# Convolution taps shared between VectorE and TensorE, norms applied two chunks at a time, and weight splits taken off GpSimd, in a six-layer transformer kernel

## The chip, the cores and the metric

The kernel runs on one core of a Trainium2 chip. The metric is device time in microseconds of one launch. Before the change three runs gave 2338.33, 2335.90 and 2334.93 us, a median of 2335.9 us. One more execution was taken with the hardware profiler; all durations below come from it.

## What is computed

256 tokens of 1024 channels pass through two blocks. The first has four layers of attention (differential, latent, dilated, differential) with a SwiGLU network each; nothing of it changes here. The second has two layers, and these are the subject. A layer, cut to what matters:

```
def token_mix(h, positions, w_in, ...):
    z = h @ w_in + b_in
    u_pool, u_conv, q, k, v, qi, ki, wi, gates = split_cols(z, IN_SIZES)
    ...
    y_pool = pool_mixer(u_pool, pool_w, pool_scale) @ w_pool_out
    y_conv = conformer_conv(u_conv, conv_dw_w, conv_dw_b, conv_ln_g, conv_ln_b, w_conv_out)
    y_attn = dsa_attention(q, k, v, qi, ki, wi) @ w_attn_out
    g = jax.nn.sigmoid(gates).reshape(B, L, 3, D_MODEL)
    merged = g[:, :, 0] * y_pool + g[:, :, 1] * y_conv + g[:, :, 2] * y_attn
    return merged @ w_o

def conformer_conv(u, dw_w, dw_b, ln_g, ln_b, w_pw):
    a, gate = jnp.split(u, 2, axis=-1)
    h = causal_dwconv(a * jax.nn.sigmoid(gate), dw_w, dw_b)   # 31 taps, 256 channels
    return jax.nn.silu(layer_norm(h, ln_g, ln_b)) @ w_pw

def conv_ffn(h, w_up, ffn_dw_w, ffn_dw_b, w_down):
    u = causal_dwconv(h @ w_up, ffn_dw_w, ffn_dw_b)           # 3 taps, 5632 channels
    gate, val = jnp.split(u, 2, axis=-1)
    return (jax.nn.silu(gate) * val) @ w_down

h = layer_norm(ALPHA * h + token_mix(h, ...), ln1_g, ln1_b)
h = layer_norm(ALPHA * h + conv_ffn(h, ...), ln2_g, ln2_b)
```

In the attention each query keeps its 64 highest-scored keys (score from 8 index heads).

## The kernel before, in words

**Layout and products.** Activations are held transposed: eight chunks of 128 channels on the partitions, 256 tokens along the free axis. Every product is made of three matmuls (`mm3`): each fp32 operand is split into a high part (rounded to the matmul's input type) and a low part (the rest), and high x high, high x low and low x high are added in PSUM. Weights come in pieces. For each piece SP's queue starts a DMA into one of 5 `raw` buffers, ScalarE copies it to `whi` (L243, the recording helper), VectorE subtracts to get `wlo` (L315); there are 6 buffers of each part. Some pieces are split by GpSimd, by an argument of `weights`.

**Order.** A scheduler gives each engine its instructions in an order fixed at build time. In the token mixer TensorE runs the main pieces in the order of the program; side steps (index scores, top-k, softmaxes, the convolution's norm) are put in a list with `later(delay)`, and are emitted when a virtual clock, which every main step advances with `tick`, has passed their due time. So the delays decide where side steps stand among the gate pieces, on all engines.

**Entry.** `normed` starts the layer: the statistics of the layer norm are ready late, so the first two weight pieces are multiplied with the un-normed input (z), and afterwards mended with the norm's scale and shift (`early`, L1247 and L1248). Meanwhile `ln_apply` (L1103) norms the eight chunks: per chunk two VectorE operations, a ScalarE copy to the high part, one VectorE operation for the low part. The bias of the norm is added to the kept x later, in the token mixer by eight ScalarE operations (at j == 2), in the FFN by eight GpSimd ones (L1149).

**Token mixer** (`token_mix`, L1304). After the entry: queries of the index (`zqi`), a packed piece with keys, values and index weights (`zb`), queries (`zq`); a bias row `bz` is fetched by ScalarE's queue for each (L1318) and added when the result leaves PSUM (L1333, L1358). Then two pieces for the pool branch, four for the convolution's input and its gate, then 20 gate pieces (j = 2 to 11, two each). Transposes of keys (`zkd`), 8 index products, 8 rounds of top-k on VectorE (L1409, L1410) and 8 softmax steps (`attend`) are side steps. The 31 taps of the convolution run on TensorE between the gate pieces j = 3 to 6: the input, padded in front (`cvp`), is shuffled so that even and odd tokens share the partitions, and each of four packed pieces of tap weights (times two halves) has 16 calls of `mm3` with 128 columns, 64 calls a layer.

**FFN** (`conv_ffn`, L1609). 22 pairs of pieces j, 48 matmuls of 256 columns for each j. The result is copied from PSUM (`upr`, ScalarE, 128x512), one ScalarE and two VectorE operations per half make the three taps (`gut`), and a product with a SiLU gives `guh`. The pieces j = 2 to 6 have one of their two splits on GpSimd.

Of the kernel before, what the change touches and what calls it, by code (L numbers as in the profile page):

```python
# [25 lines left out]
CW = 31  # L26
# [4 lines left out]
NPOOL, NH = 7, 18  # L31
# [70 lines left out]
def prepare(i):  # L102
# [39 lines left out]

    dw = f(i["conv_dw_w_2"]).reshape(2, CW, 2, 2, 64)
    tp = np.zeros((2, 2, 64, 16, 2, 2, 2, 64), np.float32)
    for e in range(2):
        for sh in range(2):
            for d in range(16):
                for o in range(2):
                    j = 2 * d + sh - o
                    if 0 <= j < CW:  # L150
                        for c in range(64):
                            tp[:, sh ^ e, c, d, :, e, o, c] = dw[:, j, :, e, c]
    a["w_tap"] = tp.reshape(2, 128, 4, 2048).transpose(0, 2, 1, 3)
# [17 lines left out]
    for l in range(2):  # L171
# [3 lines left out]
        p.add(f"psc{l}", cols(f(i["pool_scale_2"])[l]))  # L175
        p.add(f"cb{l}", cols(f(i["conv_dw_b_2"])[l]))
# [42 lines left out]
class Program:  # L219
# [153 lines left out]
    def setup(self):  # L373
# [6 lines left out]
        for h, eng in ((0, nc.sync), (1, nc.scalar)):  # L380
            x = c.tile([128, 4, 256], F32, name=f"x{h}")
            eng.dma_start(x, xv[:, 4 * h:4 * h + 4, :])
            self.x += [x[:, k, :] for k in range(4)]
        self.ident = self.col("ident", 0, 128)
# [692 lines left out]
    def spread(self, mean, sq, eps, extra=None):  # L1077
# [20 lines left out]
        ra, bb = self.t1("lna"), self.t1("lnb2")  # L1098
        self.act(ra, self.bcast(r))
        nc.vector.tensor_copy(bb, self.bcast(b))  # L1100
        return ra, bb

    def ln_apply(self, x, ra, bb, g, b):  # L1103


        xs = self.splits()
        for k in range(8):
            gk, bk = self.col(g, k), self.col(b, k)
            self.stt(x[k], x[k], gk, ra, OP.mult, OP.mult)
            self.stt(x[k], bb, gk, x[k], OP.mult, OP.add)  # L1110
            self.act(xs[k][0], x[k], AF.Identity, bias=bk)
            self.stt(xs[k][1], x[k], bk, xs[k][0].bitcast(F32), OP.add, OP.subtract)
        return xs
# [31 lines left out]

    def bias(self, b):

        for k in range(8):
            self.nc.gpsimd.tensor_scalar(self.x[k], self.x[k], self.col(b, k), None, op0=OP.add)  # L1149
# [78 lines left out]
    def normed(self, st, aps, take):  # L1228


        ra, bb = self.stats(st)
# [6 lines left out]
        xs = self.ln_apply(self.x, ra, bb, st["g"], st["b"])  # L1238
# [14 lines left out]
    def angles(self):  # L1253
# [40 lines left out]
        self.cvp = c.tile([128, 2, 287], F32, name="cvp")  # L1294
# [9 lines left out]
    def token_mix(self, l, st):  # L1304
# [111 lines left out]
        self.later(3.0, lambda: keys(0, kiT))  # L1416
        for hh in range(8):
            self.later(5.5 + 1.5 * hh, lambda hh=hh: index(hh))
        self.later(18.0, attended)
# [52 lines left out]
        wide_ = lambda: self.rslot().rearrange("p a b -> p (a b)")[:, :574].rearrange("p (f n) -> p f n", f=2)  # L1472
        nh, nl = wide_(), wide_()
        self.split(nh, nl, cvp, 1.0)
        taps = []
        for n in (nh, nl):
            o = self.rslot().rearrange("p a b -> p (a b)")[:, :572].rearrange("p (f e n) -> p f e n", f=2, e=2)
            for e in range(2):
                own, other = slice(64 * e, 64 * e + 64), slice(64 - 64 * e, 128 - 64 * e)
                self.act(o[own, :, e, :], n[own, :, 0:286:2].bitcast(F32))  # L1480
                self.act(o[other, :, e, :], n[own, :, 1:287:2].bitcast(F32))
            taps.append(o)
# [54 lines left out]
        for c in range(4):  # L1537
            es = {}
            for e in range(2):
                self.later(8.0 + 6.0 * (2 * c + e), lambda c=c, e=e, es=es: attend(c, e, es))  # L1540
# [3 lines left out]
        cv = []  # L1544
        for j in range(2, 12):
# [4 lines left out]
            if 3 <= j < 7:  # L1550
                b = j - 3
# [125 lines left out]
```

## Time and profile before

| | us |
|---|---|
| median of three runs | 2335.9 |
| the profiled execution | 2332.99 |
| its span in the profile | 2330.9 |
| TensorE busy | 2246.2 |
| VectorE busy | 1638.5 |
| ScalarE busy | 1358.0 |
| GpSimd busy | 271.8 |
| second block, first layer: z ends | at 1473.7 |
| its gates end | at 1632.2 |
| its FFN: z ends | at 1705.1 |

The clock granted to TensorE over the whole span was 0.986 of full speed. In the rows, PE is TensorE, DVE VectorE, ACT ScalarE, POOL GpSimd and SP SyncE; L12 is line 12 of the kernel. A matmul's own duration overlaps the next, so the pace is read from a chain of them (us and count). "idle before <-releaser" is the time in which the engine did nothing ahead of an instruction, and what ended it.

### The profile page before, as it was taken

To read this page: it belongs to the slowest core of one execution; us is meant where nothing else is said; L and a number is where in the kernel's file an instruction comes from. 1 tells how busy PE (TensorE), PEld (TensorE's weight loads), DVE (VectorE), ACT (ScalarE), POOL (GpSimd) and SP (SyncE) were. 2 spreads that over 40 slices of the span, in tenths; PEclk is the share of its full clock that TensorE was granted. 3 is DMA by queue.
4 is the path that set the end of the run, shared out by engine and by line. 5 is a ranking of instruction groups with operands and counts; after the bars stand their busy time and mean duration, and the time that the engine had idled before them with its cause. 6 is when DMAs were issued, how large, how long until landed. Compare 5 with 4: busy or idle time off the path is not lost.

```text
span 2330.9 us, 43099 instructions
## 1 busy us (share of the span) xinstructions
PE 2246.2 (96%) x16822; PEld 2111.3 (91%) x16822; DVE 1638.5 (70%) x2914; ACT 1358.0 (58%) x2470; POOL 271.8 (12%) x257
## 2 busy tenths in 40 slices
PE   8999998999999999999999999899999998998998
PEld 6899997899977778999978999789999997998998
DVE  6776666776556656766677767785888788578875
ACT  7764456544556656644577545565558565555763
POOL 1010012300010000100002002010152001005311
PEclk9999999999999999999999999999999999998999
DMA  6345553355554343455633656444445554443543
GB/s 231 131 156 187 157 174 112 114 191 159 185 189 137 115 140 126 151 184 159 203 128 121 203 164 195 156 145 139 161 144 197 159 190 145 154 166 123 199 157 106
DMA packets 113723, 370.12 MB, mean 159 GB/s; under 512 B 12656, under 2 KB 15856, under 8 KB 113520
## 3 DMA queue, kind: packets, MB, share of 16 engines
q1 hardware_dynamic: 111120, 363.84, 47.5%
q10 hardware_dynamic: 2256, 3.28, 0.5%
q8 instruction: 132, 2.16, 0.4%
q14 instruction: 71, 0.58, 0.1%
q0 software_dynamic: 144, 0.26, 0.1%
HBM read 366.54 MB, written 1.05 MB: 158 GB/s over the span
## 4 chain that ended last, share of the span: by engine, by line
PE 60%; DVE 7%; ACT 2%; issue 1%; DMA 1%; POOL 0%; ACTq 0%; DVEq 0%; SPq 0%; POOLq 0%
PE mm L272 51%; PE sc L272 6%; PE tp L326 2%; DVE xl L246 1%; DVE wlo L315 1%; DVE x L246 1%; ACT whi L243 1%; ACT s L243 1%; PE tp L272 1%; DMA raw<-w_zq 0%; DVE early L1248 0%; DVE score L1410 0%; PE tp L1061 0%; DMA bz<-b_z 0%; PE tp L714 0%
## 5 line engine op out<-in xcount | busy, mean ns | idle before, releaser
L315 DVE TENSOR_TENSOR wlo<-raw,whi 128x1024 fp32r<-128x1024 f32 (+3 forms) x742 | 842.4, 1139 | 374.5 <-ACT whi L243 373.2
L243 ACT ACTIVATE whi<-raw 128x1024 fp32r<-128x1024 f32 (+2 forms) x760 | 739.1, 978 | 540.2 <-PE mm L272 354.0
L272 PE MATMUL mm<-xh,whi 128*128 128x256 f32 x2496 | 710.1, 285 | 5.6 <-DVE early L1247 5.6
L272 PE MATMUL mm<-xh,wlo 128*128 128x256 f32 x2496 | 704.8, 283 | 3.9 <-DVE wlo L315 3.9
L272 PE MATMUL mm<-xl,whi 128*128 128x256 f32 x2496 | 705.0, 282 | 3.0 <-DVE xl L246 2.9
L272 PE MATMUL mm<-s,whi 128*128 128x256 f32 x2976 | 544.7, 284 | 0.0
L272 PEld LDWEIGHTS mm<-xh,whi 128*128 128x128 f32 x2496 | 474.1, 190 | 8.2 <-DVE early L1247 6.0
L272 PEld LDWEIGHTS mm<-xl,whi 128*128 128x128 f32 x2496 | 474.0, 190 | 4.6 <-DVE xl L246 4.0
L272 PEld LDWEIGHTS mm<-xh,wlo 128*128 128x128 f32 x2496 | 472.9, 190 | 5.3 <-DVE wlo L315 5.3
L272 PEld LDWEIGHTS mm<-s,whi 128*128 128x128 f32 x2976 | 465.4, 192 | 5.0 <-issue 3.8
L272 PE MATMUL mm<-s,wlo 128*128 128x256 f32 x1488 | 421.2, 284 | 0.0
L272 PEld LDWEIGHTS mm<-s,wlo 128*128 128x128 f32 x1488 | 285.3, 192 | 0.1
L272 PE MATMUL mm<-whi,xh 128*128 128x512 f32 (+3 forms) x608 | 246.1, 406 | 13.6 <-ACT whi L243 8.9
L272 PE MATMUL mm<-wlo,xh 128*128 128x512 f32 (+3 forms) x608 | 239.7, 394 | 0.2
L272 PE MATMUL mm<-whi,xl 128*128 128x512 f32 (+3 forms) x608 | 237.7, 391 | 0.0
L272 PEld LDWEIGHTS mm<-whi,xh 128*128 128x128 f32 x608 | 116.4, 192 | 36.1 <-ACT whi L243 8.9
L272 PEld LDWEIGHTS mm<-whi,xl 128*128 128x128 f32 x608 | 115.9, 191 | 22.4
L272 PEld LDWEIGHTS mm<-wlo,xh 128*128 128x128 f32 x608 | 116.1, 191 | 20.4 <-DVE wlo L315 1.8
L486 POOL TENSOR_TENSOR sqacc<-sqacc,sq 128x256 f32<-128x256 f32 x56 | 58.0, 1036 | 585.3 <-ACT sq L243 582.6
L243 ACT ACTIVATE s<-guh 128x256 fp32r<-128x256 f32 x132 | 54.8, 415 | 116.9 <-DVE guh L538 94.2
L534 DVE TENSOR_TENSOR gut<-mm,rbc 128x512 f32<-128x512 f32 x88 | 60.5, 691 | 40.1 <-PE mm L272 40.1
L246 DVE SCALAR_TENSOR_TENSOR gut<-upr,pk,gut 128x255 f32<-128x255 f32 (+1 forms) x160 | 78.4, 518 | 12.1 <-ACT gut L243 10.1
(314 smaller groups left out, 2651.5 us busy)
## 6 DMA issues: line engine op xcount, KB each, us to landing
raw<-w_gu SPq DMA_DIRECT2D x176, 512.0 KB, 4.7
raw<-w_up SPq DMA_DIRECT2D x88, 512.0 KB, 4.2
raw<-w_zs SPq DMA_DIRECT2D x60, 512.0 KB, 3.8
raw<-w_out SPq DMA_DIRECT2D x64, 384.0 KB, 3.2
raw<-w_cqk SPq DMA_DIRECT2D x48, 512.0 KB, 4.4
raw<-w_out SPq DMA_DIRECT2D x64, 320.0 KB, 2.8
raw<-w_aqk SPq DMA_DIRECT2D x32, 512.0 KB, 4.5
raw<-w_cv SPq DMA_DIRECT2D x24, 512.0 KB, 3.7
```

The lines of the kernel that those rows point to most:

```text
L243: return self.nc.scalar.activation(out, in_, func, bias=bias, scale=scale, **kw)
L246: return self.nc.vector.scalar_tensor_tensor(out, a, s, b, op0=op0, op1=op1)
L272: i = self.nc.tensor.matmul(*a, **kw)
L315: e.tensor_sub(lo, raw, hi.bitcast(F32))
L326: i = self.nc.tensor.transpose(out, in_, self.ident if ident is None else ident)
L486: self.nc.gpsimd.tensor_add(acc, acc, sq)
L534: nc.vector.tensor_mul(t, ps, rb[:, None, :].to_broadcast([128, 2, 256]))
```

## The change

Four parts.

1. **Taps.** Of the convolution's two chunks of 128 channels the first goes to VectorE: one ScalarE operation and 30 multiply-adds of 128x256 a layer, queued in threes with `later(6 + 4n)`. The second stays on TensorE, as 31 products with diagonal matrices (`w_tap`, now 4 pieces a layer for 8), 256 columns each, at j = 3 and j = 5. The shuffles to even and odd, and the eight copies that undid them, go.
2. **Norms.** `ln_apply` takes two chunks at a time: VectorE multiplies and adds 128x512, reading scale and shift from PSUM, where they had been copied out; ScalarE applies gain and bias (twice: to the high part and to x); VectorE subtracts once for both low parts. The separate bias additions (ScalarE's and GpSimd's) go.
3. **FFN.** The copy `upr` goes, the taps read PSUM; no split is done on GpSimd.
4. **Delays.** Keys at 9.0 (3.0), index head n at 11.2 + 1.3n (5.5 + 1.5n), top-k's end at 24 (18), softmax steps from 11 (8), the convolution's norm from 16 after j = 5 (3.5 after j = 6).

```diff
-        ra, bb = self.t1("lna"), self.t1("lnb2")
-        self.act(ra, self.bcast(r))
-        nc.vector.tensor_copy(bb, self.bcast(b))
-        return ra, bb
+        return self.bcast(r, b)
...
-        for k in range(8):
-            gk, bk = self.col(g, k), self.col(b, k)
-            self.stt(x[k], x[k], gk, ra, OP.mult, OP.mult)
-            self.stt(x[k], bb, gk, x[k], OP.mult, OP.add)
-            self.act(xs[k][0], x[k], AF.Identity, bias=bk)
-            self.stt(xs[k][1], x[k], bk, xs[k][0].bitcast(F32), OP.add, OP.subtract)
+        rb, bb = (ps[:, None, n:n + 256].to_broadcast([128, 2, 256]) for n in (0, 256))
+        for m, x2 in enumerate(self.x2):
+            self.nc.vector.tensor_mul(x2, x2, rb)
+            self.nc.vector.tensor_add(x2, x2, bb)
+            for to in (lambda k: xs[k][0], lambda k: self.x[k]):
+                for k in (2 * m, 2 * m + 1):
+                    self.act(to(k), self.x[k], AF.Identity, scale=self.col(g, k), bias=self.col(b, k))
+            two = slice(2 * m, 2 * m + 2)
+            self.nc.vector.tensor_sub(self.xl[:, two, :256], x2, self.xh[:, two, :256].bitcast(F32))
...
-        xs = self.ln_apply(self.x, ra, bb, st["g"], st["b"])
+        xs = self.ln_apply(rb, st["g"], st["b"])
+        rs = self.t2("lnrb")
+        self.act(rs, rb)
+        ra, bb = rs[:, :256], rs[:, 256:]
...
-        self.later(3.0, lambda: keys(0, kiT))
+        self.later(9.0, lambda: keys(0, kiT))
         for hh in range(8):
-            self.later(5.5 + 1.5 * hh, lambda hh=hh: index(hh))
-        self.later(18.0, attended)
+            self.later(11.2 + 1.3 * hh, lambda hh=hh: index(hh))
+        self.later(24.0, attended)
...
+        cv = [self.t1("cv") for _ in range(2)]
+        taps = self.rslot().rearrange("p a b -> p (a b)")[:, :572].rearrange("p (s n) -> p s n", s=2)
+        self.split(taps[:, 0, :], taps[:, 1, :], cvp[:, 1, :], 1.0)
+        wcol = lambda t: self.col(f"cw{l}", t)
+        self.act(cv[0], cvp[:, 0, 0:256], AF.Identity, scale=wcol(0), bias=self.col(f"cb{l}", 0))
+
+        def tapped(t0):
+            for t in range(t0, t0 + 3):
+                self.stt(cv[0], cvp[:, 0, t:t + 256], wcol(t), cv[0], OP.mult, OP.add)
+
+        for n in range(10):
+            self.later(6.0 + 4.0 * n, lambda n=n: tapped(1 + 3 * n))
...
-            if 3 <= j < 7:
-                b = j - 3
+            if j in (3, 5):
+                b = (j - 3) // 2
...
-                for k in range(16):
-                    d, n = 4 * b + k // 4, k % 4
-                    at = slice(d, d + 128)
-                    self.mm3(tap[:, n // 2, n % 2, :], w(k, 0), [x[:, n // 2, n % 2, at] for x in taps],
-                             d == 0 and n == 0, d == 15 and n == 3, skip_group_check=True)
-                    self.tick(0.19)
+                for k in range(16 - b):
+                    d = 16 * b + k
+                    self.mm3(tap, w(k, 0), [taps[:, n, d:d + 256] for n in range(2)], d == 0, d == CW - 1)
+                    self.tick(3 * US[256])
...
-                w = self.weights(up[l, j], 256, (nc.vector, nc.gpsimd) if j < NPOOL else None)
-                ps = self.smode2(w, xs)
-                t = self.t2("upr", (2, 256))
-                self.act(t, ps)
-                p = [t[:, f, :] for f in range(2)]
+                ps = self.smode2(self.weights(up[l, j], 256), xs)
+                p = [ps[:, f, :] for f in range(2)]
```

What the scheduler makes of it stands at three places of the second block's first layer. The first is ScalarE's queue at the entry of the token mixer, where `bz` is the bias row. Before, its DMA was issued inside the FFN of the first block:

```order
L243 ACTIVATE whi<-raw 128x640
L243 ACTIVATE gus<-gut 128x256
L243 ACTIVATE s_14432<-guh 128x256
L243 ACTIVATE whi<-raw 128x768
L243 ACTIVATE whi<-raw 128x640
L1318 DMA bz<-b_z 128x512
L243 ACTIVATE gus<-gut 128x256
```

And now, where x_74 are the last four chunks, `lnrb` scale and shift of the norm, `gb` and `shift` what mends the early pieces, and s_16819 the first gates:

```order
L236 ACTIVATE xh<-x_74,pk_122 128x256 x2
L236 ACTIVATE x_74<-x_74,pk_122 128x256 x2
L236 ACTIVATE lnrb<-tp 128x512
L236 ACTIVATE gb<-sc 128x2 x2
L236 ACTIVATE shift<-lnrb,gb 128x256 x3
L236 ACTIVATE s_16819<-early,hb 128x256 x2
L236 ACTIVATE gb<-mm 128x2
L1309 DMA bz<-b_z 128x512
```

The issue of `bz` has moved behind the norm's sixteen operations, the shifts and two of the gates.

The second place is VectorE at the end of top-k, where `mx` are the maxima of a round, `wlo` the low half of a weight piece, `cvp` the convolution's input. Before, the tail of top-k:

```order
L1410 MATCH_REPLACE score<-mx_17595,score 128x128
L1409 MAX mx_17598<-score 128x8
L315 TENSOR_TENSOR wlo<-raw,whi 128x1024
L1410 MATCH_REPLACE score<-mx_17598,score 128x256
L1469 TENSOR_SCALAR glu<-glu 128x256
L246 SCALAR_TENSOR_TENSOR score<-score,causal 128x384
L246 SCALAR_TENSOR_TENSOR cvp<-mm,pk_122,glu 128x256
L1414 TENSOR_SCALAR selb<-score 128x384
L435 TENSOR_TENSOR ropet<-qtok,rt 128x8x32
L436 TENSOR_TENSOR ropet<-qtok,rt 128x8x32
L315 TENSOR_TENSOR wlo<-raw,whi 128x1024
```

And now:

```order
L1401 MATCH_REPLACE score<-mx_17649,score 128x256
L429 TENSOR_TENSOR ropet<-qtok,rt 128x8x32
L239 SCALAR_TENSOR_TENSOR score<-score,causal 128x384
L430 TENSOR_TENSOR ropet<-qtok,rt 128x8x32
L1405 TENSOR_SCALAR selb<-score 128x384
L431 TENSOR_TENSOR qtok<-qtok,rt 128x512
L1460 TENSOR_SCALAR glu<-glu 128x256
L432 TENSOR_TENSOR qtok<-qtok,ropet 128x512
L239 SCALAR_TENSOR_TENSOR cvp<-mm,pk_122,glu 128x256
L308 TENSOR_TENSOR wlo<-raw,whi 128x1024
L447 TENSOR_TENSOR s_17695<-cvp,s_17695 128x286
```

The split of the third gate piece (j = 2), which is the `wlo` of this excerpt, now comes behind the whole of top-k, both ropes of the queries and both gated products; the split ahead of it stands 71 instructions earlier, among the index scores, so there is none inside top-k.

The third place is VectorE at the first softmax step, where `aexp` are the masked scores and `arec` the reciprocal of their sum. Before:

```order
L315 TENSOR_TENSOR wlo<-raw,whi 128x1024 x2
L446 ISA aexp,amax<-sc,selb 128x128
L446 ISA amax 128x1
L446 ISA aexp,amax<-sc,selb 128x256
L446 ISA amax 128x1
L315 TENSOR_TENSOR wlo<-raw,whi 128x1024 x2
L1511 RECIPROCAL arec<-asum 128x2
```

And now:

```order
L239 SCALAR_TENSOR_TENSOR cv<-cvp,pk_122,cv 128x256 x2
L440 ISA aexp,amax<-sc,selb 128x128
L440 ISA amax 128x1
L440 ISA aexp,amax<-sc,selb 128x256
L440 ISA amax 128x1
L239 SCALAR_TENSOR_TENSOR cv<-cvp,pk_122,cv 128x256 x5
L1503 RECIPROCAL arec<-asum 128x2
L239 SCALAR_TENSOR_TENSOR cv<-cvp,pk_122,cv 128x256
L1505 TENSOR_SCALAR aexp<-aexp,arec 128x128
```

Between mask and reciprocal, two weight splits stood at this step and five of the convolution's multiply-adds (`cv`) stand now, with a sixth ahead of the normalising.

## Rows read from the trace of the kernel before

**Rows 1.** The page, busy time, share of span, instructions.
```profile
PE 2246.2 (96%) x16822; PEld 2111.3 (91%) x16822; DVE 1638.5 (70%) x2914; ACT 1358.0 (58%) x2470; POOL 271.8 (12%) x257
```
**Rows 2.** Windows: length, busy time (count) by engine, clock, DMA share, GB/s.
```profile
1473.70:1537.60 63.90, 56.62 (x336) 49.65 (x334) 54.07 (x151) 32.23 (x56) 8.17 (x16) 0.95 0.41 136
1537.60:1632.20 94.60, 90.64 (x734) 86.05 (x735) 55.70 (x108) 60.56 (x117) 1.64 (x5) 0.98 0.49 166
1705.10:1722.50 17.40, 13.81 (x98) 12.99 (x96) 17.40 (x25) 10.33 (x22) 14.93 (x9) 0.90 0.29 99
1903.00:1964.40 61.40, 55.82 (x336) 49.68 (x334) 52.41 (x146) 31.28 (x54) 8.17 (x16) 0.97 0.43 142
1964.40:2057.90 93.50, 89.08 (x734) 85.19 (x735) 55.70 (x108) 60.68 (x117) 0.71 (x1) 1.00 0.48 167
2131.30:2149.10 17.80, 12.07 (x99) 11.46 (x97) 17.80 (x24) 9.79 (x19) 16.73 (x11) 0.97 0.29 98
1499.40:1506.20 6.80, 3.51 (x9) 2.67 (x10) 3.85 (x14) 0.76 (x2) 0.00 (x0) 0.50 0.85 264
```
**Rows 3.** Timeline of TensorE, token mixer's entry: start, us, what, idle before.
```profile
1499.53 0.45 PE L326 MATMUL tp<-pk,zkd 128*128 128x128 f32 x1 [2.28 <-DVE zkd L1361]
1503.14 0.47 PE L326 MATMUL tp<-pk,zkd 128*128 128x128 f32 x1 [3.16 <-DVE zkd L1361]
...
1537.62 0.39 PE L272 MATMUL mm<-xh,wlo 128*128 128x256 f32 x1 [0.42 <-DVE wlo L315]
```
**Rows 4.** The chain of waits in the gates: start, us, engine and line, count.
```profile
1553.31 1.29 PE sc L272 x12
...
1554.95 4.63 PE sc L272 x40
...
1623.02 9.04 PE mm L272 x76
```
**Rows 5.** Groups by form, VectorE from 1723 to 2000; last two, whole span.
```profile
L315 DVE TENSOR_TENSOR wlo<-raw,whi 128x1024 fp32r<-128x1024 f32 x65 | 81.2, 1253 | 18.7 <-ACT whi L243 18.7
L246 DVE SCALAR_TENSOR_TENSOR gut<-upr,pk,gut 128x255 f32<-128x255 f32 x40 | 20.6, 523 | 5.5 <-ACT gut L243 5.5
...
L246 DVE SCALAR_TENSOR_TENSOR x<-x,pk,lna 128x256 f32<-128x256 f32 x8 | 3.6, 474 | 0.0
...
L437 DVE TENSOR_TENSOR qtok<-qtok,rt 128x512 f32<-128x512 f32 x4 | 2.7, 681 | 0.0
L1333 DVE TENSOR_TENSOR qtok<-mm,bz 128x512 f32<-128x512 f32 x4 | 2.6, 682 | 0.0
...
L246 DVE SCALAR_TENSOR_TENSOR s<-s,mm x48: 411/414/422, 1640.5 to 2087.2; 128x256 f32<-128x256 f32 x48
...
L534 DVE TENSOR_TENSOR gut<-mm,rbc 128x512 f32<-128x512 f32 x88 | 60.5, 691 | 40.1 <-PE mm L272 40.1
```
**Rows 6.** DMA issues of the bias row: count, KB each, median us to landing.
```profile
bz<-b_z ACTq DMA_DIRECT2D x4, 256.0 KB, 5.5
```
**Rows 7.** Timeline of VectorE, top-k of the first layer.
```profile
1521.83 0.61 DVE L1409 MAX8 mx<-score 128x8 f32<-128x128 f32 x2
...
1532.83 1.20 DVE L315 TENSOR_TENSOR wlo<-raw,whi 128x1024 fp32r<-128x1024 f32 x1
...
1534.03 0.40 DVE L1410 MATCH_REPLACE8 score<-mx,score 128x256 f32<-128x256 f32 x1
```
**Rows 8.** Timeline of TensorE, third pair of pieces (j = 4), both FFNs.
```profile
1722.51 0.39 PE L272 MATMUL mm<-xh,whi 128*128 128x256 f32 x1 [0.95 <-DVE early L1247]
...
2149.09 0.58 PE L272 MATMUL mm<-xh,whi 128*128 128x256 f32 x1 [4.62 <-DVE early L1247]
```
**Rows 9.** Timelines of VectorE and GpSimd, early pieces of the first FFN.
```profile
1716.65 2.54 DVE L246 SCALAR_TENSOR_TENSOR gut<-early,pk,gut 128x254 f32<-128x254 f32 x1
1719.11 2.62 DVE L1248 TENSOR_TENSOR early<-early,shift 128x256 f32<-128x256 f32 x1
...
1716.54 4.91 POOL L315 TENSOR_TENSOR wlo<-raw,whi 128x1024 fp32r<-128x1024 f32 x2
```

## What the change does to the time, predicted

> **What bounds the kernel now.** I read the page first: TensorE is busy for 96% of the span [rows 1], so a gain has to take work or idle time from it, and the other engines count only where it waits for them. The change leaves the first four layers alone, so the table by stretches comes next, with one row for each stretch of the second block that the change touches [rows 2]. In each row the reader is to take the length and TensorE's busy time. Entry of the token mixer: 63.90 us with 56.62 busy in its first layer, 61.40 with 55.82 in its second. Gates: 94.60 with 90.64, and 93.50 with 89.08. The two early pieces of the FFN: 17.40 with 13.81, and 17.80 with 12.07. So gates are bound by TensorE's work, and entries by what it waits for. [...] When the third gate piece starts, at 1537.62, it waits only 0.42 us for its low half: top-k has just let VectorE go.
>
> **The taps.** Before, a layer has 64 calls of three matmuls of 128 columns, 192. In the chain of waits 12 take 1.29 us and 36 of them with 4 score products 4.63 us [rows 4]: 107 and 116 ns each; at 113 ns, 21.7 us a layer. After, the second chunk has 31 calls, 93 matmuls of 256 columns. 76 of that width take 9.04 us [rows 4], 119 ns each, so 93 take 11.1 us. The first chunk costs TensorE nothing. **Gain 10.6 us a layer**, all on the path, since TensorE bounds the gates; bounds 192 x 0.107 - 93 x 0.121 = 9.3 and 192 x 0.116 - 11.1 = 11.2. So half the columns cost nine tenths of the time, and the change halves the number of matmuls. [...]
>
> VectorE pays for the first chunk with 30 operations of 128x256 a layer. They read SBUF, as the FFN's tap operations do (523 ns [rows 5]) and the norm's (474 ns [rows 5]): 30 x 0.42 to 0.5, 12.6 to 15 us. The gates have VectorE busy for 55.70 of 94.60 us [rows 2]; four tap pieces fewer take 4 x 1.25 off [rows 5], so it comes to 63 to 66 of some 84 us. That fits, if nothing urgent stands behind the new ones. Something does: in the changed order five and then one of them stand between a softmax's mask and its normalising. About 2.4 us come into a chain that needs some 1.4 us without them; TensorE has 42 matmuls, 5 us, before it asks for the result. Cost taken: nothing; the cover lasts until the return is over 1.3 us later still.
>
> **The entry of the token mixer.** TensorE's own work is the busy time less what half clock adds: 56.62 - 1.8 (3.51 busy us at 0.50, [rows 2]) = 54.9 us, and about as much in the second layer. What it lost was 9.0 us and 6.5 us. These waits go: the keys, due at 9 for 3, are transposed after 39 of the 48 matmuls that stand there, so the 2.28 and 3.16 us have cover.
>
> Three waits come. (a) ScalarE issues the DMA of the bias row behind sixteen norm operations, where it had been issued in the FFN before. From issue to landing is 5.5 us [rows 6]. [...] (b) Behind the two additions (682 ns each [rows 5]) VectorE does seven rope operations before it splits the next weights: 3.1 us. (c) **Top-k.** From its first maximum (1521.83) to its last replacement (1534.43) VectorE takes 12.6 us, with one weight split of 1.20 us inside [rows 7]. In the changed order no split stands there: eight rounds with the small ropes (12.6 - 1.2 = 11.4), both halves' query ropes (each two operations of 681 ns [rows 5] and two of half that size, 4.0), then the split (1.2); the two gated products, masks and last scores I put at 3 (some nine operations of 0.25 to 0.5, the norm's 474 ns being the nearest row [rows 5]): 19 to 20 us after the last index product. TensorE has 105 matmuls and six transposes until it wants that split, 13.3 us. Wait 6.4 us; from 3, if the scores come early, to 8. Behind each of the two longer waits I put a half-clock stretch as the row shows it, 1.8 us lost.
>
> So the entry takes 54.9 + 2.6 + 3.1 + 6.4 + 3.6 = 70.6 us, against 63.9 and 61.4: **a loss of 6.7 and 9.2 us**. Bounds for a layer: 60 (waits 3 in all) and 76.
>
> **The norms.** For two chunks VectorE had six operations of 474 ns [rows 5], of which 0.08 overlaps the next, and now has three of 128x512; the nearest row with a PSUM operand is 691 ns [rows 5]. Eight chunks: 12 x 0.65 = 7.8 for 24 x 0.4 = 9.6 us. ScalarE gets eight more, about 0.4 us each, beside them. In the token mixer this lies in the entry above. In the FFN the third piece pair (j = 4) starts 17.4 and 17.8 us after the end of z [rows 2], having waited 0.95 and 4.62 us [rows 8], for 96 matmuls that need 11.5. Two VectorE operations there take 2.54 and 2.62 us while GpSimd splits weights for 4.91 us [rows 9], where such operations take 474 to 523 ns [rows 5]; that goes with the split on GpSimd, some 4.2 us. Put back on VectorE, each split costs 1.25 us [rows 5], and the one for j = 4 stands in the changed order behind twelve tap operations. Norm to 1708.6, early pieces and taps 9 us, split: ready at 1718.9, for 1722.51. **Gain 3.2 us an FFN**, after 0.4 for a longer half clock; bounds nothing and 5.9.
>
> **The FFN's other pieces.** The copy of 128x512 out of PSUM goes from ScalarE, and four tap operations read PSUM themselves. An operation with a PSUM operand of that size (`s<-s,mm`) takes 414 ns [rows 5], less than the 523 ns from SBUF, so no price. Per piece VectorE has two splits, four taps and a product, some 5 us at most, under TensorE's 48 x 0.12 = 5.8. Taken: nothing; it lasts until VectorE needs 0.8 us more a piece. [...]
>
> **Sum.** Taps 2 x 10.6 = 21.2, entries -15.9, FFNs +6.4: 11.7 us. The half-clock stretches were added to the waits as if they never fell on idle time; I give 1.8 us of the 7.2 back, which makes 13.5. The profiled execution takes 2333.0 us, so 2319.5; the median of the three runs is 2.9 us above it, 2335.9, and the forecast for the median is **2322 us**.
>
> **Rivals.**
> *Waits smaller.* The 105 matmuls under top-k hold transposes of late keys and queries; if TensorE's work there covers VectorE after all, (c) and its half clock fall away in both layers: 2 x 8.2 = 16 us more, 2306; with (a) gone too, 2300. For it: 0.42 us of wait before. Against it: there the scores came 6 us earlier, and one split stood inside.
> *Gain given back.* The order is moved but TensorE's starts are bound as before: the taps' 21 us are eaten by entries at their upper bound (76 us: 12 and 15 us lost). 21.2 + 6.4 - 27 = 0.6: 2335. That includes the case that the change does nothing.
> *VectorE bounds the gates: slower.* Place: the tap operations between mask and normalising. Price: above 1.3 us of delay every microsecond is TensorE's in each of the 16 softmax chains, eight a layer. If six more operations of 0.5 us, with one split of 1.25, stand before the result, it is 4.2 - 1.3 = 2.9 us a chain, 46 us in all; with half of the chains hit, 23: 2336 + 23 - 13.5 = 2345. It takes over from 0.85 us a chain on. For it: VectorE goes from 59% to 77% of the stretch. Against it: 5 us of cover and 18 us of idle.
>
> **Chances.** No change I call within 0.2% (4.7 us), about what a measurement can tell. The forecast has 0.50 (2312 to 2331), smaller waits 0.26 (2296 to 2312), gain given back 0.15 (2331 to 2341), VectorE the bound 0.09 (above 2341). Faster 0.76, same 0.15, slower 0.09. The range leaves out the better half of a case on top and the slower one: 2302 to 2336.
>
> **What would show it.** The tap groups: 186 matmuls of 256 columns at 119 ns. Entry rows: transposes of the keys with no wait, a wait for the bias row's addition, and one of 5 to 7 us for the low half at the third gate piece. Gates: 82 to 86 us. FFN pieces: j = 4 starts 14 us after z. The prediction is wrong in its largest term if the entry is shorter than 64 us, and in kind if TensorE waits in the gates for softmax results.

## The result, and the profile after

The changed kernel takes **2312.26 us** (median of 4 runs, 2311.30 to 2312.77), against 2335.99 (4 runs): a ratio of 0.9897, 95% interval 0.9879 to 0.9914, so 1.0% faster, 23.7 us. The forecast was 2322 with a range of 2302 to 2336: the sign and the range held, and the gain was under-estimated, 13.9 us forecast. The median lies at the better edge of the forecast's own band (2312 to 2331), 10 us from its middle. The profiled execution of the changed kernel took 2312.77 us with a span of 2310.9, 20.0 under the span before. The two executions do not start the second block together: the first block, which is the same in both, ended 0.6 us later after the change. So the stages are compared one by one.

Busy time, from the page of the changed kernel:

```profile
PE 2225.8 (96%) x16624; PEld 2094.2 (91%) x16624; DVE 1629.7 (71%) x2924; ACT 1325.3 (57%) x2410; POOL 225.5 (10%) x231
```

TensorE's busy time fell by 20.4 us, which is all of the span's gain. VectorE's barely moved [rows 1]: it does 60 multiply-adds more in the two layers (28.8 us) and ten splits that GpSimd did before, but eight tap splits fewer, and its norms in fewer operations.

The same stretches as in [rows 2], from the windows of the changed kernel (length, busy time and count by engine, clock, DMA share, GB/s): entry, gates and early FFN pieces of the first layer, then of the second.

```profile
1474.33:1540.67 66.34, 56.05 (x341) 50.47 (x339) 56.91 (x153) 36.90 (x65) 8.61 (x16) 0.95 0.37 126
1540.67:1623.36 82.69, 80.72 (x631) 77.54 (x632) 57.07 (x125) 47.60 (x94) 2.66 (x5) 0.96 0.48 166
1695.34:1711.32 15.98, 12.36 (x100) 11.74 (x98) 13.79 (x30) 15.98 (x36) 1.56 (x2) 1.00 0.03 9
1893.10:1959.20 66.10, 55.37 (x341) 48.83 (x339) 56.53 (x151) 35.88 (x60) 8.61 (x16) 0.99 0.42 136
1959.20:2042.46 83.26, 81.29 (x631) 78.23 (x632) 57.16 (x125) 47.47 (x94) 1.79 (x1) 0.95 0.47 165
2113.81:2129.33 15.52, 12.20 (x100) 11.73 (x99) 13.32 (x30) 15.52 (x35) 1.56 (x2) 0.97 0.02 8
```

The lengths, first in each row, are to be compared. The gates are 11.9 and 10.2 us shorter, the entries 2.4 and 4.7 longer, the early FFN pieces 1.4 and 2.3 shorter. In the early FFN pieces ScalarE is now busy for the whole stretch (15.98 of 15.98), where VectorE was before.

TensorE's waits that answer to [rows 3] and [rows 8], from its timeline (start, duration, what, idle before it and what ended that):

```profile
1490.28 0.64 PE L265 MATMUL mm<-wlo,xh 128*128 128x328 f32 x1 [2.73 <-DVE wlo L308]
1506.94 0.38 PE L319 MATMUL tp<-pk,zkd 128*128 128x128 f32 x2
1540.67 0.58 PE L265 MATMUL mm<-xh,wlo 128*128 128x256 f32 x1 [6.26 <-DVE wlo L308]
1711.32 0.39 PE L265 MATMUL mm<-xh,wlo 128*128 128x256 f32 x1 [3.14 <-DVE wlo L308]
...
1959.20 0.58 PE L265 MATMUL mm<-xh,wlo 128*128 128x256 f32 x1 [6.25 <-DVE wlo L308]
2129.33 0.58 PE L265 MATMUL mm<-xh,wlo 128*128 128x256 f32 x1 [3.13 <-DVE wlo L308]
```

The transposes of the keys wait for nothing in this layer now; in the second layer one of them waits 1.1 us. The third gate piece waits 6.26 us for its low half, the wait (c) of the prediction, and j = 4 of the FFN 3.14. Top-k on VectorE shows why (same view, VectorE):

```profile
1522.05 0.61 DVE L1400 MAX8 mx<-score 128x8 f32<-128x128 f32 x2
...
1535.87 0.40 DVE L1401 MATCH_REPLACE8 score<-mx,score 128x256 f32<-128x256 f32 x1
...
1539.01 0.47 DVE L239 SCALAR_TENSOR_TENSOR cvp<-mm,pk,glu 128x256 f32<-128x256 f32 x1
1539.40 1.21 DVE L308 TENSOR_TENSOR wlo<-raw,whi 128x1024 fp32r<-128x1024 f32 x1
```

From the first maximum to the last replacement it is 14.2 us, where [rows 7] had 12.6 with a split inside; ropes, masks and gated product follow, and only then comes the split that TensorE waits for. Behind it, in the gates of the first layer, TensorE's only wait of over 0.3 us is 2.0 us for a product of the pool branch (`pp`), and that was 1.9 before.

### The profile page after: what moved, and what is told of

It is laid out like the page before. It is cut to its first block, busy times and chain, and to the rows that moved or that the text cites. A ratio compares the mean times of both kernels' runs of the same rounds, so it can differ in the third digit from the quotient of the medians.

```text
span 2310.9 us, 42575 instructions
## 1 busy us (share of the span) xinstructions
PE 2225.8 (96%) x16624; PEld 2094.2 (91%) x16624; DVE 1629.7 (71%) x2924; ACT 1325.3 (57%) x2410; POOL 225.5 (10%) x231
## 4 chain that ended last, share of the span: by engine, by line
PE 61%; DVE 6%; ACT 3%; issue 1%; POOL 0%; DMA 0%; ACTq 0%; DVEq 0%; POOLq 0%
PE mm L265 53%; PE sc L265 5%; PE tp L319 2%; DVE wlo L308 1%; ACT whi L236 1%; DVE xl L239 1%; ACT xh L236 1%; ACT x L236 0%; PE tp L265 0%; DVE score L1401 0%; PE tp L1055 0%; PE tp L708 0%; DVE mx L1400 0%; DVE gut L239 0%; DVE acc L1044 0%
## 5 line engine op out<-in xcount | busy, mean ns | idle before, releaser
L308 DVE TENSOR_TENSOR wlo<-raw,whi 128x1024 fp32r<-128x1024 f32 (+2 forms) x744 | 840.5, 1134 | 357.7 <-ACT whi L236 354.5
L236 ACT ACTIVATE whi<-raw 128x1024 fp32r<-128x1024 f32 (+3 forms) x752 | 731.3, 978 | 574.8 <-PE mm L265 375.3
L236 ACT ACTIVATE s<-tp 128x512 fp32r<-128x512 f32 (+4 forms) x96 | 50.3, 524 | 62.1 <-PE tp L819 25.6
```

The costliest lines, as they stand in the source:

```text
L236: return self.nc.scalar.activation(out, in_, func, bias=bias, scale=scale, **kw)
L308: e.tensor_sub(lo, raw, hi.bitcast(F32))
```

## The experiments

All comparisons are with the kernel before on the same chip. The four parts of the change were first put alone on the kernel before; in the diffs, code that stands in the change's diff is not repeated. The two stage columns are from each profiled execution, first and second layer: the mixer from the end of z to the first product behind the convolution's norm, and the FFN from the end of z to the sum that starts the next norm.

| kernel | median us | ratio, 95% interval | mixer us | FFN us |
|---|---|---|---|---|
| before | 2335.99 | | 165.5, 161.9 | 153.4, 156.3 |
| the change | 2312.26 | 0.9897 [0.9879, 0.9914] | 156.1, 156.4 | 153.2, 153.8 |
| taps_alone | 2309.03 | 0.9880 [0.9862, 0.9899] | 152.3, 154.3 | 156.0, 153.7 |
| norms_alone | 2335.74 | 1.0006 [0.9993, 1.0019] | 167.0, 171.1 | 151.7, 151.7 |
| ffn_alone | 2338.73 | 1.0011 [1.0001, 1.0021] | 166.8, 166.8 | 156.2, 153.2 |
| delays_alone | 2332.51 | 0.9979 [0.9964, 0.9993] | 163.5, 161.4 | 154.7, 153.5 |
| whole_old_delays | 2314.56 | 0.9900 [0.9885, 0.9916] | 153.4, 152.9 | 153.0, 153.2 |
| whole_splits_ahead | 2309.92 | 0.9885 [0.9871, 0.9900] | 152.4, 156.0 | 152.9, 153.0 |
| taps_splits_ahead | 2306.42 | 0.9877 [0.9861, 0.9894] | 151.7, 149.9 | 153.4, 153.5 |
| both_chunks_on_tensore | 2332.50 | 0.9980 [0.9971, 0.9990] | 163.0, 162.8 | 156.0, 156.4 |
| all_taps_on_vectore | 2302.36 | 0.9864 [0.9847, 0.9880] | 151.2, 149.6 | 153.3, 153.3 |
| taps_order_mended | 2310.63 | 0.9895 [0.9881, 0.9910] | 152.8, 152.7 | 153.4, 153.5 |
| whole_again | 2312.58 | 0.9907 [0.9892, 0.9921] | 156.1, 152.6 | 153.2, 153.2 |
| taps_again | 2308.25 | 0.9890 [0.9875, 0.9905] | 152.1, 152.2 | 153.4, 153.7 |

The profiled execution of norms_alone took some 7 us more than that kernel's median, so its stages are to be read with care.

**taps_alone**: the tap hunks of the change (`prepare`, the tap loop, `tapped`), delays as before but for the convolution's norm, which goes to its new place.

```diff
+        for n in range(10):
+            self.later(6.0 + 4.0 * n, lambda n=n: tapped(1 + 3 * n))
...
-            if 3 <= j < 7:
+            if j in (3, 5):
```

> Only the taps of the change, at the old delays (the convolution's norm at its new place). Theory: the whole gain in the gates is 192 matmuls of 128 columns against 93 of 256, 10.6 us a layer, with nothing lost at the entry: 21 us under the kernel before, about 2315. Rival: the taps on VectorE stand in the softmax chains, which start 3 us earlier here than in the changed kernel, and TensorE waits for them: a gain under 12 us, 2324 or more.

Measured: 26.3 us under the kernel before. The taps are the whole gain and more; the theory's 21 us is what the mixers show (13.2 and 7.6, so 20.8). The other 5 us are not assigned to a cause here; both_chunks_on_tensore, below, gives 3 us for the packed form of the taps. The rival has nothing for it: after the third gate pair TensorE waits there for two things only, and no softmax result is among them (its waits, us in total, times, longest):

```profile
PE sc L266 <- DVE pp L240: 2.1, 1, 2.1
PE mm L266 <- DVE wlo L309: 1.1, 1, 1.1
```

**norms_alone**: the hunks in `spread`, `ln_apply` and `normed`, and the bias operations taken out.

```diff
-        xs = self.ln_apply(self.x, ra, bb, st["g"], st["b"])
+        xs = self.ln_apply(rb, st["g"], st["b"])
...
-            if j == 2:
-                for k in range(8):
-                    self.act(self.x[k], self.x[k], AF.Identity, bias=self.col(st["b"], k))
```

> Only the norms two chunks at a time. Theory: ScalarE's sixteen operations of 0.5 us set the norm's end now, 8 us, where VectorE's 24 took 10 to 11; the entries gain 1 to 2 us each, and the bias operations cost nothing before: 3 to 6 us under the kernel before, 2330 to 2333. Rival: the early pieces stand behind the norm on ScalarE and eat it: no change, 2336.

Measured: no change. The low parts wait for ScalarE now, as the rows of VectorE in this kernel's FFN entry show:

```profile
1714.77 0.69 DVE L1112 TENSOR_TENSOR xl<-x,xh 128x512 fp32r<-128x512 f32 x1 [0.69 <-ACT x L243]
1716.74 0.69 DVE L1112 TENSOR_TENSOR xl<-x,xh 128x512 fp32r<-128x512 f32 x1 [1.27 <-ACT x L243]
```

The expected pace of ScalarE was right (from one of these rows to the next are 1.97 us, in which it does four operations, so 0.49 each); that it would be a gain in the median was not. The late norm is not the whole reason, though. Both FFNs of this execution are the shortest of all kernels here, 151.7 us for 153.4 and 156.3 before; its mixers are 1.5 and 9.2 us longer. In the first layer's entry a wait of 2.73 us for a low half is new, the same as in the changed kernel, so that wait comes with the norms and not with the delays. The second mixer has a granted clock of 0.88 to 0.96 in its first three quarters; why it is so low is not shown.

**ffn_alone**:

```diff
-                w = self.weights(up[l, j], 256, (nc.vector, nc.gpsimd) if j < NPOOL else None)
+                w = self.weights(up[l, j], 256, None)
                 ps = self.smode2(w, xs)
-                t = self.t2("upr", (2, 256))
-                self.act(t, ps)
-                p = [t[:, f, :] for f in range(2)]
+                p = [ps[:, f, :] for f in range(2)]
```

> Only the FFN part: no copy out of PSUM, no split on GpSimd. Theory: the two stretched VectorE operations (2.54 and 2.62 us) go, but the splits come back on VectorE in front of the same matmuls; 2 to 3 us an FFN, 2330 to 2332. Rival: the splits on VectorE are later than GpSimd's were: no change or up to 4 us slower.

Measured: 0.1% slower, at the edge of what can be told; the rival's case. TensorE's largest wait at the first FFN is now this one, where [rows 8] had 0.95; at the second it is 3.23, where [rows 8] had 4.62. So one FFN lost what the other gained:

```profile
1727.93 0.58 PE L272 MATMUL mm<-xh,wlo 128*128 128x256 f32 x1 [4.76 <-DVE wlo L315]
```

**delays_alone**:

```diff
-        self.later(3.0, lambda: keys(0, kiT))
+        self.later(9.0, lambda: keys(0, kiT))
...
-            self.later(5.5 + 1.5 * hh, lambda hh=hh: index(hh))
-        self.later(18.0, attended)
+            self.later(11.2 + 1.3 * hh, lambda hh=hh: index(hh))
+        self.later(24.0, attended)
...
-                self.later(8.0 + 6.0 * (2 * c + e), lambda c=c, e=e, es=es: attend(c, e, es))
+                self.later(11.0 + 6.0 * (2 * c + e), lambda c=c, e=e, es=es: attend(c, e, es))
```

> Only the delays of keys, index scores, top-k's end and softmax steps. Theory: the waits for the keys go (5 us in the first layer, 4 in the second), a wait of about 6 us and a half-clock stretch behind top-k come, and the later softmax steps save some 2 us a layer: between 2 us faster and 6 us slower, 2334 to 2342. Rival: the delays bring the part of the gain above the taps, 4 to 6 us faster, 2330 to 2332.

Measured: 2332.51, 0.2% faster, just past the better end of the theory's range and short of the rival's, with single runs from 2326.08 to 2337.47; it does not decide between them. The trade of waits is as expected: those for the keys go, and this one comes, the same as in the changed kernel:

```profile
1542.75 0.58 PE L272 MATMUL mm<-xh,wlo 128*128 128x256 f32 x1 [6.25 <-DVE wlo L315]
```

The four ratios add up to -1.24% (-1.20, +0.06, +0.11, -0.21), the whole to -1.03%. That the parts together cost something which none of them costs alone is a suspicion only: the difference of 0.21% is smaller than what the five intervals leave open. The next runs follow it up.

**whole_old_delays**: the changed kernel with the diff of delays_alone undone.

> The changed kernel with the four delays of the kernel before. The taps alone gave 26 us and the whole gives 24, so the other parts cost something together. Theory: it is the wait of 6.5 us for the split behind top-k and the half clock after it, 8 us a layer, which the new delays made; against it come back the waits for the keys (5 us) and for the first softmax steps (0 to 2). About 2 us a layer better: 2306 to 2310. Rival: the norm on ScalarE and the FFN's splits cost it, and the delays are right for them: 2312 to 2318.

Measured: 2314.56, in the rival's range; three of the four runs are between 2314.26 and 2315.39, so by the medians the theory missed, and the old delays win nothing back. The profiled execution was the fourth, 2308.67, and in it the mixers take 153.4 and 152.9 us, as with the taps alone. What the delays cost is left open.

**whole_splits_ahead**: from the changed kernel,

```diff
-        self.later(9.0, lambda: keys(0, kiT))
+        self.later(6.0, lambda: keys(0, kiT))
...
-            self.later(11.2 + 1.3 * hh, lambda hh=hh: index(hh))
-        self.later(24.0, attended)
+            self.later(8.2 + 1.3 * hh, lambda hh=hh: index(hh))
+        self.later(21.0, attended)
...
+        wc2 = [self.weights(i["w_zs"][l, 1 + f], 256) for f in range(2)]
         for f in range(2):
-            w = self.weights(i["w_zs"][l, 1 + f], 256)
+            w = wc2[f]
+            if f == 1:
+                w2 = self.weights(i["w_zs"][l, 5], 256)
             ps = self.smode2(w, xs)
...
-            w = self.weights(i["w_zs"][l, 3 + j], 256)
+            w = w2 if j == 2 else self.weights(i["w_zs"][l, 3 + j], 256)
```

> The changed kernel with keys at 6, index scores from 8.2, top-k's end at 21, and the weight pieces of the convolution's second half and of the third gate piece asked for one piece ahead, so that their splits stand after rounds 4 and 8 of top-k. Theory: the wait of 6.5 us becomes under 1.5, the half clock behind it goes, and TensorE's next waits are the query transposes (1 us): 5 to 7 us a layer, 2298 to 2303. Rival: VectorE has as much to do as before and is only asked in another order, so TensorE waits as long a few pieces later: 2309 to 2313.

Measured: 2309.92, 2 to 3 us under the changed kernel, within the rival's range; the intervals of the two ratios overlap. At the split TensorE's starts are 2.8 us apart for 6.5 before, and a gap of 2.1 us for the first query transpose came behind it, in both layers: part of the wait moved on, as the rival has it.

**taps_splits_ahead**: the same edit on the taps alone, so keys from 3.0 to 6.0, index heads from 5.5 + 1.5n to 8.2 + 1.3n, top-k's end from 18 to 21, and the lines with `wc2` and `w2`.

> The taps alone on the kernel before, with keys at 6, index scores from 8.2, top-k's end at 21 and the same two splits ahead. Theory: the waits for the keys (2.0 and 3.6 us, 2.6 and 2.6) and for the split behind top-k (1.4 and 2.1) fall to under 2 together: 4 to 6 us a layer under the taps alone, 2298 to 2302. Rival: the keys' transposes wait for VectorE's splits wherever they stand: no gain, 2307 to 2311.

Measured: 2306.42, with single runs from 2301.86 to 2310.81; below the taps alone by some 2 us (1.8 and 2.6 under its two medians), less than the spread. The keys are waited for once (2.3 us) instead of twice, and two more waits are left on TensorE's timeline:

```profile
1533.59 0.38 PE L266 MATMUL mm<-xh,wlo 128*128 128x256 f32 x1 [2.50 <-DVE wlo L309]
...
1537.20 0.44 PE L320 MATMUL tp<-pk,qtok 128*128 128x128 f32 x2 [1.80 <-DVE qtok L432]
```

**taps_order_mended** asks for the third and fourth gate pieces earlier still (before and right after the convolution's second half), turns the queries 2 us later and starts the softmax steps at 11.

```diff
-            self.later(5.0, lambda: turn(qT, toks[t], t, -0.125))
+            self.later(7.0, lambda: turn(qT, toks[t], t, -0.125))
...
+        w2 = self.weights(i["w_zs"][l, 5], 256)
...
             ps = self.smode2(w, xs)
+            if f == 1:
+                w3 = self.weights(i["w_zs"][l, 6], 256)
...
-            w = w2 if j == 2 else self.weights(i["w_zs"][l, 3 + j], 256)
+            w = (w2, w3)[j - 2] if j < 4 else self.weights(i["w_zs"][l, 3 + j], 256)
```

> The taps with splits ahead, where waits of 2.8 us for a low half and 2.1 us for the first query transpose were left in each layer: the third gate piece is asked for one more piece ahead, the fourth as well, the queries are transposed 2 us later and the softmax steps start at 11. Theory: VectorE's urgent work is then in the order in which TensorE asks for it, 3 to 5 us a layer go: 2297 to 2301. Rival: VectorE's queue is full from the first score to the fourth gate piece, and the wait only moves behind it: 2303 to 2308.

Measured: 2310.63. A miss, beyond the rival too: the two waits of 2.50 and 1.80 became one of 5.17, in each layer.

```profile
1543.22 0.69 PE L320 MATMUL tp<-pk,qtok 128*128 128x128 f32 x2 [5.17 <-DVE qtok L432]
```

In the 28 us up to the end of this wait VectorE is busy all the time (27.95 of 28.00 us, 1515 to 1543), and what is put ahead of one thing stands behind another.

**both_chunks_on_tensore**: taps alone, with the first chunk as diagonals too (`w_tap` of two chunks; `tapped` and its ScalarE start taken out; the convolution's norm follows j = 6 in place of j = 5).

```diff
-            if j in (3, 5):
-                b = (j - 3) // 2
+            if 3 <= j < 7:
+                g, b = (j - 3) // 2, (j - 3) % 2
...
-                    self.mm3(tap, w(k, 0), [taps[:, n, d:d + 256] for n in range(2)], d == 0, d == CW - 1)
+                    self.mm3(tap, w(k, 0), [taps[g][:, n, d:d + 256] for n in range(2)], d == 0, d == CW - 1)
```

> Both chunks as diagonals of 256 columns on TensorE, nothing on VectorE: 62 products, 186 matmuls a layer, at the kernel-before's delays (the convolution's norm as with the taps alone). Theory: the gain of the taps is TensorE's time alone, and 186 x 0.119 = 22.1 us are no less than 192 x 0.113 = 21.7: no change, 2333 to 2338. Rival: part of the gain is the shuffles and copies that the packed form needed on ScalarE, and the waits that they made: 2322 to 2330.

Measured: 3.3 us faster, 0.2%, just past the theory's range and far from the taps' 26. So most of the gain is the half that TensorE no longer does. The narrower count, 186 for 192, and the packing are worth 3 us at most. The chain of waits of this kernel confirms the price of wide taps, 5.64 us for 46 products, nearly all of them taps, so 123 ns each:

```profile
1552.59 5.64 PE sc L267 x46
```

**all_taps_on_vectore**: taps alone, with the second chunk on VectorE as well; the convolution's norm follows j = 7 in place of j = 5.

```diff
         def tapped(t0):
             for t in range(t0, t0 + 3):
-                self.stt(cv[0], cvp[:, 0, t:t + 256], wcol(t), cv[0], OP.mult, OP.add)
+                for g in range(2):
+                    self.stt(cv[g], cvp[:, g, t:t + 256], wcol(g, t), cv[g], OP.mult, OP.add)
...
-                self.act(cv[1], tap, AF.Identity, bias=self.col(f"cb{l}", 1))
```

> The taps alone, but both chunks on VectorE: 60 multiply-adds a layer, none on TensorE. TensorE's gates lose another 93 x 0.119 = 11.1 us a layer and come to some 72; VectorE's rise by 30 x 0.4 to 0.48 less the four splits of the tap pieces (5 us), to 63 to 67 of them, over 90%. Theory (VectorE was not near its limit with one chunk, and is with two): the softmax returns wait for it, half or more of the 22 us is given back, 2292 to 2305. Rival 1: it is all hidden, 2287. Rival 2 (my slower rival, VectorE bounds the gates): slower than with one chunk, over 2309.

Measured: **2302.36 us**, the fastest kernel here, 10 us under the changed one and about 6 under the taps alone. TensorE has 22 us less to do in the two layers, and the mixers show 3.5 to 5.8 us of it (300.8 in all, against 306.6 and 304.3). The rest, about three quarters, is in two places. One is new waits, some 4 to 5 us a layer more than with one chunk: for the low halves of two gate pieces, and for ScalarE behind the convolution's norm (TensorE's timeline):

```profile
1544.09 0.38 PE L263 MATMUL mm<-xh,wlo 128*128 128x256 f32 x1 [1.92 <-DVE wlo L306]
...
1569.26 0.39 PE L263 MATMUL mm<-xh,wlo 128*128 128x256 f32 x1 [2.39 <-DVE wlo L306]
...
1622.98 0.39 PE L263 MATMUL mm<-cc,whi 128*128 128x256 f32 x1 [1.76 <-ACT cc L234]
```

The other is that TensorE's matmuls took longer: from the first of these waits (1544.09; 1547.41 in taps_again) to the first product behind the convolution's norm its busy time was 72.60 us for 78.62 in taps_again, and 71.42 for 78.60 in the second layer, where 11.1 us of work had gone from each. The clock shows it in the first layer, 0.95 in this stretch, while with one chunk it was 1.00 (windows of this kernel, then of taps_again); in the second layer it was 0.98, against 1.00 in taps_again and 0.96 in taps_alone, so what set it is not shown:

```profile
1544.00:1616.00 72.00, 67.58 (x519) 63.95 (x520) 58.13 (x141) 40.20 (x85) 2.29 (x5) 0.95 0.48 156
```

```profile
1547.41:1621.60 74.19, 71.94 (x583) 68.92 (x584) 52.49 (x119) 45.62 (x92) 3.09 (x5) 1.00 0.52 171
```

VectorE is busy for 81% of it, against 71%. TensorE waits for it more than before, but the kernel is still faster.

**whole_again** and **taps_again**, the changed kernel and the taps alone on one chip, side by side.

> The changed kernel itself once more, on the same chip as the next, to tell whether its other three parts cost something. Theory (the wait behind top-k and its half clock are given away by the new delays): 2 to 5 us above the taps alone. Rival: the two are the same within 1 us, and the difference so far was the chip's.

> The taps alone once more, beside the changed kernel on the same chip: 2 to 5 us below it by the theory, within 1 us by the rival.

Measured: 2312.58 and 2308.25, 4.3 us apart; the intervals of their ratios overlap in part (0.9892 to 0.9921, 0.9875 to 0.9905). In the first layer's mixer both executions of the whole are some 4 us above the taps (156.1 twice, against 152.3 and 152.1); in the second's one is above (156.4 against 154.3 and 152.2) and one is not (152.6). With both pairs of medians on the same side I take the other three parts to cost 3 to 4 us together. That it is the wait behind top-k is supported by the first layer, where both edits that shorten it bring the mixer to 152.4 and 153.4; the medians of those kernels don't settle it. The second layer of whole_again speaks against it: the same wait of 6.26 us, and a mixer of 152.6. A rival is the wait of 2.73 us (1.1 and 0.8 in the second layer) that came with the norms, and it was not tried on its own. The cause stays open.

## Why the prediction was right, point by point

- **Taps, 10.6 us a layer: right.** The gates are 11.9 and 10.2 us shorter. Two things that the term left out are in these numbers and pull opposite ways, so the close match is in part luck: waits of 2.0 and 2.5 us for index scores and query transposes, which stood in the gates before, are gone from there, and the gates' clock is lower (below). The price itself is shown by the chain. In the chain of waits of the changed kernel 36 tap matmuls of 256 columns take 4.28 us, 119 ns each, as predicted from gate matmuls:

```profile
1554.91 4.28 PE sc L265 x36
```

- **Taps on VectorE at nothing: right.** 57.07 of 82.69 us busy, less than the 63 to 66 predicted: the 30 multiply-adds cost 14.4 us, as put, but some 4 us of query ropes and gated product moved into the entry (56.91 us busy there, for 54.07). No start of TensorE in the gates is held up by a softmax result for as much as 0.3 us. The slower rival would need VectorE to be late in those chains; twice as many taps brought waits for weight splits, but none over 0.3 us for a softmax result (all_taps_on_vectore).
- **Wait (c), 6.4 us: right, 6.26 and 6.25.** It was read off the order: 20 us of VectorE against 13.3 of TensorE. Measured from the last index product, about 1519.3, it was 21.3 (split done at 1540.61) against 15.1 (TensorE ready at 1534.41): each side 1.3 to 1.8 us longer than counted, 1.3 of TensorE's by waits for a key and a query transpose that the count had left out. So the mechanism held, and the last tenths are luck.
- **Wait (a), 2.6 us: wrong.** No run shows the 2.6 us that the sum has for it. ScalarE issued the DMA at 1481.07, and VectorE used the row at 1484.36, so it landed within 3.3 us, where I took the 5.5 of [rows 6]. TensorE asked for the PSUM bank that the first addition frees only after its 48 matmuls of 512 columns, which took from 1474.33 to 1485.44, 0.231 us each. With the row in time, (a) cost nothing (ScalarE's queue, then VectorE, up to the split that ends wait (b)):

```profile
1481.07 0.33 ACTq L1309 DMA_DIRECT2D bz<-b_z  x1
```

```profile
1484.36 0.68 DVE L1324 TENSOR_TENSOR qtok<-mm,bz 128x512 f32<-128x512 f32 x1
1485.64 0.69 DVE L1324 TENSOR_TENSOR qtok<-mm,bz 128x512 f32<-128x512 f32 x1 [0.59 <-PE mm L265]
...
1489.39 0.83 DVE L308 TENSOR_TENSOR wlo<-raw,whi 128x656 fp32r<-128x656 f32 x1
```

- **Wait (b), 3.1 us: right, 2.73** in the first layer, with the seven rope operations between the two additions and the split; in the second TensorE waits there 1.1 us for ScalarE and 0.8 for VectorE.
- **The half clock, 3.6 us a layer: too much at the entry.** The clock is 0.95 and 0.99 over the entries, where 0.95 and 0.97 stood before [rows 2]; the gates have 0.96 and 0.95, for 0.98 and 1.00. Around wait (c) of the first layer it is 0.82 from 1532 to 1541, where TensorE mostly waits, and 0.73 in the 7.3 us behind the wait, which are in the gates. So a part falls on the wait itself, where it costs nothing, and the rest into the gates. With (a), this is why the entries took 66.3 and 66.1 us and not 70.6: 7.1 us lost in all, not 15.9. Those 8.8 us are the largest error of the sum, and it goes towards too small a gain; the FFNs gave 3.7 us less than predicted, which goes the other way. That the total stayed as near as 20.2 us measured for 13.5 forecast (profiled executions) is partly luck. The rest is small: the gates gave 0.9 us more, 1.8 of the half clock had been given back already, and the stretches from the gates to the FFN, at nothing in the sum, are 0.9 and 2.0 us shorter.
- **FFNs, 3.2 us each: wrong in its step.** j = 4 starts 1.4 and 2.3 us earlier (15.98 and 15.52 us after z, where 14 was put), and TensorE still waits 3.1. The step that failed is "ScalarE gets eight more, about 0.4 us each, beside them": sixteen operations at 0.5 us are 7.9 us in a row, and the norm ends when they do, with VectorE waiting for them. It ends at 1701.9, 6.6 us after z, where I had 3.5 (from the changed kernel's timeline):

```profile
1699.25 0.69 DVE L1105 TENSOR_TENSOR xl<-x,xh 128x512 fp32r<-128x512 f32 x1 [0.68 <-ACT x L236]
1701.22 0.69 DVE L1105 TENSOR_TENSOR xl<-x,xh 128x512 fp32r<-128x512 f32 x1 [1.28 <-ACT x L236]
```

  The two FFNs together are 2.7 us shorter, against 6.4 predicted. With the norms alone they are 6.3 us shorter, though the norm there waits for ScalarE too. TensorE's waits at j = 4 are then three, 0.91, 1.75 and 0.73 us, and the clock in the 27.8 us from the end of z on is 1.00; in the changed kernel, where GpSimd does no split and j = 4's stand on VectorE behind the taps, the wait is one of 3.14 us, and the clock over the same length is 0.94. That the FFN part takes back what the norms gain there is likely, but it rests on one execution of norms_alone.
- **PSUM reads at no price: right.** The 160 tap operations of the two FFNs take a median of 478 ns with an operand in PSUM (`mm`, changed kernel) and 483 ns with all in SBUF (`upr`, kernel before). The prediction's 523 ns was a mean that held some of the operations stretched beside GpSimd (up to 966 ns; one of 0.95 us starts at 1733.91, while GpSimd is at work from 1732.87 to 1734.59), so its margin was too wide, but the sign holds.

## What to carry to other kernels

Work taken off the engine that bounds a stretch was worth its price here for as long as that engine went on to bound it: the first chunk of taps, moved to an engine that was idle for 40% of the stretch, came out at its price (10.6 us a layer put, the gates 11.9 and 10.2 us shorter); of the second chunk's 22 us about a quarter was seen. The sum for the first can be made from two rows, one for each width of matmul. When an order is available, count what stands in a queue between the last input and the instruction that others wait for: that count gave a wait of 6.4 us that was measured as 6.26. Try the parts of a change one by one: here one of four carried all of the gain, and both chunks of taps on VectorE without the other three parts were 10 us faster than the change. And look at the stages of a part that shows no gain: in the one execution profiled, the norms gained in the FFNs and lost in the mixers.

## What the runs showed of the hardware that was not expected

The first block is the same in all of these kernels, and yet the sum before its last norm starts between 1426.9 us (taps_alone) and 1433.5 us (norms_alone) of the span: over 6 us of spread from code that did not change. Medians of kernels that lie 2 or 3 us apart contain this spread too. Some of the spread goes with the clock. The second mixer of the changed kernel took 156.5 us in one execution and 152.9 in another (whole_again), with the same wait of 6.3 us before the third gate piece; TensorE's busy time for it was 143.79 us at a granted clock of 0.97, and 141.36 at 0.98:

```profile
1892.70:2049.20 156.50, 143.79 (x1031) 134.20 (x1030) 117.70 (x278) 87.53 (x160) 10.39 (x17) 0.97 0.45 152
```

```profile
1893.30:2046.20 152.90, 141.36 (x1033) 132.19 (x1032) 117.69 (x278) 87.86 (x161) 10.40 (x17) 0.98 0.46 155
```

A wait of 1.1 us for a key transpose stands in the first of them alone; the 2.4 us of busy time are for the same work. So a difference of 3 us in a single stage of a single execution is no evidence here, and the medians are to be read with their intervals.
